# Modulation on four column groups of TensorE, its gate part beside the last tokens, norms one group ahead

## The chip, the cores and the metric

The kernel runs on one core of one Trainium2 chip. The core has five engines with their own instruction streams: TensorE (PE in the profile; its weight loads are listed apart as PEld), VectorE (DVE), ScalarE (ACT), GpSimd (POOL) and SyncE (SP). In this kernel SP issues all the transfers between the chip's memory and the core's SBUF. The metric is the time of one execution on the device, in microseconds; a time is the median of several executions. Each engine works through its stream in order, and an instruction that waits holds up all that stand behind it on its engine.

## What is computed

One layer of a streaming encoder, for 2048 prompt tokens and 8 sample streams of 16 tokens with a cache of 512 each, all of width 1024. Cut to what the change touches:

```python
def adaln_modulate(x, c, norm_g, w_ada, b_ada):
    mod = c @ w_ada + b_ada
    shift, scale, gate = jnp.split(mod, 3, axis=-1)
    h = rms_norm(x, norm_g) * (1.0 + scale[:, None, :]) + shift[:, None, :]
    return h, gate[:, None, :]

h, gate = adaln_modulate(xp, c_prompt, norm_g[l], w_ada[l], b_ada[l])
qa, ka, va, za, qb, kb, vb, zb, ga, gb = project_inputs(h, w_in[l], pos_p)
...
xp = xp + gate * merge_branches(oa, ob, za, zb, ga, gb, ...)
```

Here `c` has 9 rows (one for the prompt, eight for the sample streams), and `w_ada` is 1024 by 3072. Shift and scale (the first 2048 columns) are needed before any token can be projected. The gate (the last 1024) is used only where the output is made, at the end of the layer. Between the two stand the projections, differential attention and stick-breaking attention, and the merge.

## The kernel before

The program has an opening, a long loop and an output stage. The loop runs over 8 units (a unit is one head of differential attention, or two of stick-breaking attention) and over 17 tiles of 128 tokens, of which tile 16 is the sample tokens. For each step it projects one tile with the unit's weights and scores an earlier one. The projection's matmuls form one long list, `line`; `take(target, need)` cuts off the next pieces of it, and `interleave` merges several lists of pieces by their costs.

What is written in the program is a priority, not yet the order that runs. A planner at build time (`schedule_with_timeline_sim=True`) puts each engine's instructions in order by this priority and by when it expects them to be ready, and hands out the buffers of a pool as they come free. So the trace shows some work well ahead of its place in the program: the weights of unit 1 (`wst`, line 298) are requested at 32.83 us, while the opening runs until 160 us.

The opening (lines 875 to 1076) makes the modulated tokens in five groups: `GROUPS` 0 to 3 of 512 prompt tokens, and group 4 of the 128 sample tokens.

- Lines 903 to 910: the 9 rows of `c` are turned by TensorE so that their 1024 features lie on the partitions, and copied to `cT`, 8 blocks of 128 by 9. `bgT` has the biases and norm weights, turned in the same way.
- `modulation(n, p)`, lines 912 to 923: makes 512 columns of `c @ w_ada`. The weights come in two loads of 1 MB into `wide` buffers. There are 6 of those (`WIDE_BUFS`), and they hold the tokens, too: two tiles of 128 tokens to a buffer. Per half, 8 matmuls with `cT[:, k, :]` as the stationary operand add up into 9 rows of an accumulator bank. VectorE copies the 9 rows out, and four small transposes put them back with features on the partitions, into the bank `p`.
- Lines 925 to 936: `modulation` for n = 0 to 2, then loads and scales of unit 0's weights, then n = 3, then the loads of the tokens of groups 4 and 0 (`load_x`, line 893).
- Lines 938 to 994: factors of the attention and, from the modulation's first four blocks, the table `ab` of factors and offsets (lines 972 to 974), and a common scale `sh` (line 991) from their sizes.
- `normed(g)`, lines 996 to 1007: loads the group's tokens, ACT squares and adds up each tile (`sum_squares`, line 251), VectorE takes the root (`rsqrt`, lines 227 to 244: three rounds of four small steps), and GpSimd multiplies each tile by it in place (line 1007).
- `modulated(g)`, lines 1009 to 1041: eight pieces, one for each block of 128 features. TensorE transposes up to four tiles (line 1022), ACT (line 1028) and VectorE (line 1029) apply `ab` into a high part and a full one, and GpSimd or VectorE takes the difference for the low part (line 1037). With the last piece the group is stored to `hT_d` (line 1039); the copy in SBUF, `hp`, serves the first projections (`at_hand`).
- `gates()`, lines 1043 to 1066: `modulation` for n = 4 and 5 and then the gate's rows, turned back and stored to `gate_d` (line 1057). The output stage reads them from there (line 1214).
- Lines 1068 to 1076 set the order: norms of groups 4 and 0, group 4, then group 0 with `gates()` beside it, then the norm of group 1, and for groups 1 to 3 each group beside projections of unit 0 (up to tile positions `P0_AT`), and after it the norm of the next.

After the opening its pool is closed, and the loop's score buffers take over its memory.

Of the kernel before, what the change touches and what calls it, by code (L numbers as in the profile page):

```python
# [16 lines left out]
F32 = mybir.dt.float32  # L17
# [29 lines left out]
P0_AT = 2.0, 4.0, 6.0  # L47
# [45 lines left out]
def interleave(*streams):  # L93

    order = []
    for i, pieces in enumerate(streams):
        lo, hi = 0.0, 1.0
        if isinstance(pieces, tuple):  # L100
            pieces, lo, hi = pieces
        total = sum(cost for cost, _ in pieces) or 1.0
        done = 0.0
        for j, (cost, fn) in enumerate(pieces):
            order.append((lo + (hi - lo) * (done + cost / 2) / total, i, j, fn))
            done += cost
    for _, _, _, fn in sorted(order, key=lambda e: e[:3]):
        fn()
# [3 lines left out]
def layer_kernel(ctx: ExitStack, tc: tile.TileContext, a: dict):  # L112
    nc = tc.nc
    V, S, G, T = nc.vector, nc.scalar, nc.gpsimd, nc.tensor
# [112 lines left out]
    def rsqrt(sums, n, width, pool, name):  # L227

        m, tag = (4, "rs") if n <= 4 else (n, f"rs{n}")
        kw = {} if n <= 4 else dict(bufs=1)  # L230
        q = tiny.tile([P, m], F32, tag=tag + "_q", name="rs_q", **kw)[:, 0:n]
        V.tensor_scalar(out=q, in0=sums, scalar1=1.0 / width, scalar2=EPS, op0=ALU.mult, op1=ALU.add)
        i = tiny.tile([P, m], I32, tag=tag + "_i", name="rs_i", **kw)[:, 0:n]
        V.tensor_scalar(out=i, in0=q.bitcast(I32), scalar1=1, scalar2=None, op0=ALU.logical_shift_right)
        y = pool.tile([P, m], I32, tag=name, name=name)[:, 0:n]
        V.tensor_scalar(out=y, in0=i, scalar1=-1.0, scalar2=1597463007.0, op0=ALU.mult, op1=ALU.add)
        y = y.bitcast(F32)
        t = tiny.tile([P, m], F32, tag=tag + "_t", name="rs_t", **kw)[:, 0:n]
        for _ in range(3):
            V.tensor_tensor(out=t, in0=y, in1=y, op=ALU.mult)  # L240
            V.tensor_tensor(out=t, in0=t, in1=q, op=ALU.mult)  # L241
            V.tensor_scalar(out=t, in0=t, scalar1=-0.5, scalar2=1.5, op0=ALU.mult, op1=ALU.add)
# [612 lines left out]
    def position(x):  # L855

        m = min(int(x), len(steps) - 1)
        return starts[m] + (starts[m + 1] - starts[m]) * (x - m)

    def take(target, need):  # L860

        i = at[0]
        out = []
        while i < len(line) and (i < target or any(m <= need for m, _ in line[i : i + 14])):
            out.append((1.0, line[i][1]))
            i += 1
        at[0] = i
        return out
# [5 lines left out]
    ab = con.tile([P, 2, KT, 9], F32, name="ab")  # L874
    with tc.tile_pool(name="p0", bufs=1) as p0:
# [27 lines left out]
        pt = bank("t")  # L903
        for k in range(KT):
            T.transpose(pt[:, k * 16 : k * 16 + 9], cs[0:9, k * P : (k + 1) * P], ident[0:9, 0:9])
        T.transpose(pt[:, 128:160], bg, ident[0:32, 0:32])
        cT = p0.tile([P, KT, 9], F32, name="cT")
        V.tensor_copy(out=cT, in_=pt[:, 0 : KT * 16].rearrange("p (k r) -> p k r", r=16)[:, :, 0:9])
        bgT = p0.tile([P, 32], F32, name="bgT")
        V.tensor_copy(out=bgT, in_=pt[:, 128:160])  # L910

        def modulation(n, p):

            pw = bank("mm")
            for i in range(2):
                wa = wide_tile()
                load(out=wa, in_=w_ada[:, :, n * 512 + i * 256 : n * 512 + (i + 1) * 256])
                for k in range(KT):
                    T.matmul(pw[0:9, i * 256 : (i + 1) * 256], cT[:, k, :], wa[:, k, :], start=(k == 0), stop=(k == KT - 1))
            ms = p0.tile([P, 512], F32, tag="tmp", name="tmp", bufs=2)  # L920
            V.tensor_copy(out=ms[0:9, :], in_=pw[0:9, :])
            for j in range(4):
                T.transpose(p[:, j * 16 : j * 16 + 9], ms[0:9, j * P : (j + 1) * P], ident[0:9, 0:9])

        pm = bank("o")
        xs = {}
        for n in range(3):
            modulation(n, pm[:, n * 64 : (n + 1) * 64])
# [3 lines left out]
        modulation(3, pm[:, 192:256])  # L932
        for fn in early[4:] + late0:
            fn()
        xs[4] = load_x(16, 1)
# [28 lines left out]
        pmv = pm[:, 0:256].rearrange("p (j r) -> p j r", r=16)  # L964
# [7 lines left out]
        V.tensor_tensor(out=ab[:, 0, :, :], in0=pmv[:, 8:16, 0:9], in1=wide(b1), op=ALU.add)  # L972
        V.tensor_tensor(out=ab[:, 0, :, :], in0=ab[:, 0, :, :], in1=wide(bgT[:, 24:32]), op=ALU.mult)
        V.tensor_tensor(out=ab[:, 1, :, :], in0=pmv[:, 0:8, 0:9], in1=wide(bgT[:, 0:8]), op=ALU.add)

        mcol = p0.tile([P, 2], F32, name="mcol")
        V.tensor_reduce(out=mcol[:, 0:1], in_=ab[:, 0, :, :].rearrange("p k r -> p (k r)"), axis=AX.X, op=ALU.max,
# [16 lines left out]
                        scalar1=sh[:, 0:1], scalar2=None, op0=ALU.mult)  # L994

        def normed(g):

            t0, w = GROUPS[g]
            nt = w // P
            ss = p0.tile([P, 4], F32, tag="ss", name="ss", bufs=2)  # L1000
            if g not in xs:
                xs[g] = load_x(t0 // P, nt)
            for i, x in enumerate(xs[g]):
                sum_squares(x, D, ss[:, i : i + 1])
            rstd = rsqrt(ss[:, 0:nt], nt, D, p0, "rstd")
            for i, x in enumerate(xs[g]):
                G.tensor_scalar(out=x, in0=x, scalar1=rstd[:, i : i + 1], scalar2=0.0, op0=ALU.mult, op1=ALU.add)

        def modulated(g):

# [31 lines left out]

        def gates():

            box = {}

            def last():
                gateT = p0.tile([P, KT, 9], F32, name="gateT")
                V.tensor_tensor(out=gateT, in0=box["p"][:, 0:128].rearrange("p (j r) -> p j r", r=16)[:, :, 0:9],
                                in1=wide(bgT[:, 16:24]), op=ALU.add)  # L1050
# [6 lines left out]
                load(out=gate_d, in_=gr[0:9, 0:D])  # L1057

            def piece(n):
                if n == 4:  # L1060
                    box["p"] = bank("t")
                modulation(n, box["p"][:, (n - 4) * 64 : (n - 3) * 64])
                if n == 5:
                    last()

            return [(1.0, lambda n=n: piece(n)) for n in (4, 5)]

        normed(4)
        normed(0)
        interleave(modulated(4))  # L1070
        interleave(modulated(0), gates())
        normed(1)
        for g in range(1, 4):
            interleave(modulated(g), take(position(P0_AT[g - 1]), -1))
            if g < 3:
                normed(g + 1)


    at_hand.clear()
# [260 lines left out]
```

## Time and profile before

| | |
|---|---|
| time, median of 3 runs | 2507.16 us (2504.18 to 2513.22) |
| the profiled execution | 2508.37 us |
| its span, first to last instruction | 2506.5 us |
| TensorE busy | 2195.5 us, 88% of the span |
| VectorE busy | 1793.3 us, 72% |
| ACT busy | 1602.7 us, 64% |
| GpSimd busy | 827.6 us, 33% |
| DMA engines' share, queue 1 | 76.6% |
| mean granted clock of TensorE | 0.940 |

A share of busy time is an average over the stages of the run, and a busy TensorE is not TensorE at its peak, as its matmuls are pipelined. A row of a view by line gives the line, engine and operation, what is written and read, shapes and count; behind the first bar stand the busy time and the mean length of one (ns), behind the second the idle time before and what ended it. A row of a view in order of time begins with the start and the length in us, and its bracket gives the idle time before it and what ended that. A row of a view by windows gives a stretch, its length, each engine's busy time with its instructions, the granted clock, the DMA share and GB/s.

### The profile page before, as it was taken

Reading aid. Unit: us, or ns where it says so; the run is one execution under the profiler, and the core shown is the slowest. Engines: PE = TensorE matmul, PEld = TensorE weight load, DVE = VectorE, ACT = ScalarE, POOL = GpSimd, SP = SyncE. Lnnn points to the kernel's source line nnn. Section 1 sums busy time; section 2 is a strip of 40 time slices with the busy share of each in tenths; the row PEclk is TensorE's granted clock in tenths of the full one; section 3 lists DMA queues with packets and bytes.
Section 4 is the critical chain, followed back from the end, with each engine's and each line's share of the span. In section 5 each row is a group of like instructions: output and inputs, shape, how many; then the busy total and the mean of one; then the engine's idle time right before and its main releaser. Section 6 shows DMA issues by size and latency. Waiting matters only on the chain. (4 is left out here: it accounts for less than half of the span.)

```text
span 2506.5 us, 45283 instructions
## 1 busy us (share of the span) xinstructions
PE 2195.5 (88%) x16366; PEld 1275.3 (51%) x16366; DVE 1793.3 (72%) x3762; ACT 1602.7 (64%) x3200; POOL 827.6 (33%) x671
## 2 busy tenths in 40 slices
PE   7859898899999988889989888999975788889997
PEld 3435555455655555556655555555543344444443
DVE  3577846877676678757577876656787888888765
ACT  2558757787767688657678876656775545445542
POOL 1543113354211244311034442102344454544422
PEclk8979999999999999999999999999985799899999
DMA  9578878998787899767679976656678989888531
GB/s 287 183 221 206 211 175 200 196 220 191 180 193 185 198 222 212 172 152 183 157 192 194 219 190 177 160 132 142 153 168 206 257 224 242 242 212 229 167 111 51
DMA packets 890994, 477.07 MB, mean 190 GB/s; under 512 B 540074, under 2 KB 842330, under 8 KB 890256
## 3 DMA queue, kind: packets, MB, share of 16 engines
q1 hardware_dynamic: 890768, 474.17, 76.6%
q8 instruction: 128, 2.10, 0.4%
q14 instruction: 98, 0.80, 0.1%
HBM read 272.94 MB, written 73.44 MB: 138 GB/s over the span
## 5 line engine op out<-in xcount | busy, mean ns | idle before, releaser
L409 PE MATMUL ps_mm<-wpair,hg 128*128 128x512 f16 x3120 | 789.7, 388 | 58.1 <-DMA hg<-hT_d 54.4
L594 POOL TENSOR_TENSOR sc_p<-sc_p,sc_n 128x127 f32<-128x127 f32 (+7 forms) x192 | 314.0, 1639 | 807.3 <-DVE sc_n L588 796.0
L409 PEld LDWEIGHTS <-hg 128*128 128x128 f16 x3120 | 281.9, 100 | 328.9 <-DMA hg<-hT_d 62.5
L476 PE MATMUL ps_t<-gw,hg 128*128 128x256 f16 (+1 forms) x2856 | 397.6, 293 | 2.3 <-DVE qst L504 2.3
L476 PEld LDWEIGHTS <-hg 128*128 128x128 f16 x2856 | 280.4, 100 | 96.0 <-DVE qst L504 2.6
L588 DVE TENSOR_TENSOR_SCAN sc_n<-ps_s,sc_n,zero_t 128x512 f32<-128x512 f32 x192 | 245.6, 1279 | 63.4 <-ACT ps_s L121 58.2
L611 PE MATMUL ps_s<-k,qst 128*128 128x512 f16 (+3 forms) x640 | 226.5, 355 | 53.3 <-DVE sc_n L588 41.2
L545 DVE TENSOR_TENSOR sc_n<-sc_p,sc_n 128x128 f16<-128x128 f32 (+7 forms) x192 | 229.7, 1201 | 39.2 <-ACT sc_n L544 38.8
L121 ACT ACTIVATE sc_p<-ps_s,usc 128x512 f32<-128x512 f32 (+3 forms) x320 | 205.0, 641 | 47.1 <-PE ps_s L612 25.6
L612 PE MATMUL ps_s<-k,qst 128*128 128x512 f16 (+3 forms) x640 | 226.3, 356 | 0.0
L1227 PE MATMUL ps_mm<-wb,uT 128*128 128x512 f16 x816 | 206.8, 407 | 20.5 <-DVE o L1125 12.5
L121 ACT ACTIVATE ps_s<-ps_s,usc 128x512 f32<-128x512 f32 (+3 forms) x328 | 199.9, 610 | 0.0
L1266 PE MATMUL ps_o<-wo,yT 128*128 128x512 f16 x816 | 193.0, 390 | 6.9 <-ACT wo L269 2.4
L663 PE MATMUL ps_o<-v,wt 128*128 128x128 f16 x1088 | 156.5, 226 | 39.8 <-DMA wt<-sc_n 39.7
L544 ACT CAST sc_n<-sc_p 128x128 f16<-128x128 f32 (+7 forms) x192 | 154.8, 813 | 49.5 <-POOL sc_p L594 48.7
L442 POOL TENSOR_TENSOR rot<-pr,rope 128x256 f32<-128x256 f32 x68 | 59.8, 879 | 351.8 <-ACT pr L423 293.7
L251 ACT ACTIVATE junk<-wst 128x1024 f16<-128x1024 f32 x124 | 131.6, 1062 | 47.2 <-DMA wst<-in_w_in_dram 17.4
L663 PEld LDWEIGHTS <-wt 128*128 128x128 f16 x1088 | 104.0, 102 | 90.3 <-DMA wt<-sc_n 49.7
L1227 PEld LDWEIGHTS <-uT 128*128 128x128 f16 x816 | 82.7, 104 | 125.3 <-issue 50.8
L530 DVE TENSOR_SCALAR_CACHE_REDUCE sc_n<-ps_s,usc 128x512 f32<-128x512 f32 (+3 forms) x160 | 106.6, 666 | 55.2 <-PE ps_s L615 34.2
L664 PE MATMUL ps_o<-v,wt 128*128 128x64 f16 x1088 | 145.2, 198 | 0.0
L530 DVE TENSOR_SCALAR_CACHE_REDUCE sc_p<-ps_s,usc 128x512 f32<-128x512 f32 (+3 forms) x160 | 106.5, 666 | 52.6 <-PE ps_s L612 41.7
(295 smaller groups left out, 4372.9 us busy)
## 6 DMA issues: line engine op xcount, KB each, us to landing
hg<-hT_d SPq DMA_DIRECT2D x130, 512.0 KB, 4.5
wst<-in_w_in_dram SPq DMA_DIRECT2D x112, 256.0 KB, 3.8
g<-g_d SPq DMA_DIRECT2D x34, 512.0 KB, 5.8
wst<-in_w_in_dram SPq DMA_DIRECT2D x32, 512.0 KB, 4.8
out_dram<-pr SPq DMA_DIRECT2D x204, 64.0 KB, 2.3
g_d<-gt SPq DMA_DIRECT2D x102, 128.0 KB, 3.1
wide<-in_w_ada_dram SPq DMA_DIRECT2D x12, 1024.0 KB, 10.3
z_d<-pr SPq DMA_DIRECT2D x136, 64.0 KB, 1.8
```

Of the source, the lines that this page charges most:

```text
L121: i = S.activation(**kw)
L409: T.matmul(box["p"], box["h"][:, hi, k, :], U["w"][k][:, wi, :], start=(n == 0), stop=(n == 3 * KT - 1))
L476: T.matmul(box["g"][:, 0:gw], box["h"][:, hi, k, :], U["wg"][k // per][:, k % per, wi, :], start=(j == 0), stop=(j == 3 * KT - 1))
L530: V.tensor_scalar(out=dst[:, lo : lo + n], in0=p[:, 0:n], scalar1=sc_pos, scalar2=None, op0=ALU.mult, op1=ALU.max, accum_out=job["mx"][:, ...
L545: V.tensor_tensor(out=lo, in0=src, in1=hi, op=ALU.subtract)
L588: V.tensor_tensor_scan(out=dst[:, lo : lo + n][:, ::-1], data0=src[:, 0:n][:, ::-1], data1=zero_t[:, 0:1].to_broadcast([P, n]), initial=fi ...
L594: G.tensor_tensor(out=p[:, 0:m], in0=p[:, 0:m], in1=n[:, 1 : m + 1], op=ALU.mult)
L611: T.matmul(p[:, 0:n], qst[:, c, :], kk[:, c, 0:n], start=True, stop=False)
L612: T.matmul(p[:, 0:n], qst[:, 2 + c, :], kk[:, c, 0:n], start=False, stop=not diag)
L663: T.matmul(po[:, c * P : (c + 1) * P], wt[:, wj, :], vt[:, c, :, :], start=first, stop=False)
L1227: T.matmul(pb, st["u"][:, ui * 8 + br * 4 + k, :], wb[:, br, wi, k, c], start=(n == 0), stop=(n == 11))
L1266: T.matmul(po, st["y"][:, yi * 8 + k, :], wo[:, wi, k, c], start=(n == 0), stop=(n == 3 * KT - 1))
```

## The change

- `cT` gets 32 columns in each block instead of 9, the others zero (a memory set ahead of the copy).
- `modulation(n)` spreads the 8 matmuls of a half over four groups of 32 columns of TensorE: block k goes to group k % 4, so two matmuls add up in each group, and the bank holds four partial sums below one another. VectorE copies all 128 rows; four full transposes follow, into a bank of their own; and a VectorE reduction adds the four partial sums into the new tile `mod`, from which `ab` and the gate are then read. The bank `pm` that held the blocks is gone.
- `gates()` goes from beside group 0 to beside group 3.
- `normed(g)` returns pieces (a square for each tile, with the root after the last, then a multiplication for each tile) instead of issuing them. They are interleaved with the group ahead: group 1's norm with the pieces of group 0, and so on. `gates()` takes that place beside group 3.

```diff
-        cT = p0.tile([P, KT, 9], F32, name="cT")
-        V.tensor_copy(out=cT, in_=pt[:, 0 : KT * 16].rearrange("p (k r) -> p k r", r=16)[:, :, 0:9])
+        cT = p0.tile([P, KT, 32], F32, name="cT")
+        V.memset(cT, 0.0)
+        V.tensor_copy(out=cT[:, :, 0:9], in_=pt[:, 0 : KT * 16].rearrange("p (k r) -> p k r", r=16)[:, :, 0:9])
...
+        mod = p0.tile([P, 24, 9], F32, name="mod")
+
-        def modulation(n, p):
+        def modulation(n):
...
-                    T.matmul(pw[0:9, i * 256 : (i + 1) * 256], cT[:, k, :], wa[:, k, :], start=(k == 0), stop=(k == KT - 1))
+                    T.matmul(pw[k % 4 * 32 : k % 4 * 32 + 32, i * 256 : (i + 1) * 256], cT[:, k, :], wa[:, k, :], start=(k < 4), stop=(k >= 4))
             ms = p0.tile([P, 512], F32, tag="tmp", name="tmp", bufs=2)
-            V.tensor_copy(out=ms[0:9, :], in_=pw[0:9, :])
+            V.tensor_copy(out=ms, in_=pw)
+            pt = bank("s")
             for j in range(4):
-                T.transpose(p[:, j * 16 : j * 16 + 9], ms[0:9, j * P : (j + 1) * P], ident[0:9, 0:9])
-
-        pm = bank("o")
+                T.transpose(pt[:, j * P : (j + 1) * P], ms[:, j * P : (j + 1) * P], ident)
+            V.tensor_reduce(out=mod[:, 4 * n : 4 * n + 4, :], in_=pt.rearrange("p (j g r) -> p j r g", g=4, r=32)[:, :, 0:9, :],
+                            axis=AX.X, op=ALU.add)
...
-            for i, x in enumerate(xs[g]):
-                sum_squares(x, D, ss[:, i : i + 1])
-            rstd = rsqrt(ss[:, 0:nt], nt, D, p0, "rstd")
-            for i, x in enumerate(xs[g]):
-                G.tensor_scalar(out=x, in0=x, scalar1=rstd[:, i : i + 1], scalar2=0.0, op0=ALU.mult, op1=ALU.add)
+            return [(0.5, lambda i=i: square(i)) for i in range(nt)] + [(1.0, lambda i=i: scale(i)) for i in range(nt)]
...
-        normed(4)
-        normed(0)
+        interleave(normed(4))
+        interleave(normed(0))
         interleave(modulated(4))
-        interleave(modulated(0), gates())
-        normed(1)
+        interleave(modulated(0), normed(1))
         for g in range(1, 4):
-            interleave(modulated(g), take(position(P0_AT[g - 1]), -1))
-            if g < 3:
-                normed(g + 1)
+            beside = normed(g + 1) if g < 3 else gates()
+            interleave(modulated(g), beside, take(position(P0_AT[g - 1]), -1))
```

In the new `normed`, `square(i)` and `scale(i)` hold the same instructions as the two loops did, with the root behind the last square. In `gates()`, `box["p"]` and its reading are replaced by `mod[:, 16:24, :]`.

More of the change, by code (lines that the diff above doesn't have):

```diff
@@ L931, in layer_kernel @@
             fn()
-        modulation(3, pm[:, 192:256])
+        modulation(3)
         for fn in early[4:] + late0:
@@ L963, in layer_kernel @@
         V.tensor_scalar(out=g8, in0=g8, scalar1=1.0 - LAM_INIT, scalar2=None, op0=ALU.mult)
-        pmv = pm[:, 0:256].rearrange("p (j r) -> p j r", r=16)
         b1 = p0.tile([P, 8], F32, name="b1")
@@ L970, in wide @@
             return x.unsqueeze(2).to_broadcast([P, KT, 9])
-        V.tensor_tensor(out=ab[:, 0, :, :], in0=pmv[:, 8:16, 0:9], in1=wide(b1), op=ALU.add)
+        V.tensor_tensor(out=ab[:, 0, :, :], in0=mod[:, 8:16, :], in1=wide(b1), op=ALU.add)
         V.tensor_tensor(out=ab[:, 0, :, :], in0=ab[:, 0, :, :], in1=wide(bgT[:, 24:32]), op=ALU.mult)
-        V.tensor_tensor(out=ab[:, 1, :, :], in0=pmv[:, 0:8, 0:9], in1=wide(bgT[:, 0:8]), op=ALU.add)
+        V.tensor_tensor(out=ab[:, 1, :, :], in0=mod[:, 0:8, :], in1=wide(bgT[:, 0:8]), op=ALU.add)
         mcol = p0.tile([P, 2], F32, name="mcol")
@@ L999, in normed, with square, scale @@
             nt = w // P
-            ss = p0.tile([P, 4], F32, tag="ss", name="ss", bufs=2)
+            box = {}
+            def square(i):
+                if i == 0:
+                    box["ss"] = p0.tile([P, 4], F32, tag="ss", name="ss", bufs=2)
+                sum_squares(xs[g][i], D, box["ss"][:, i : i + 1])
+                if i == nt - 1:
+                    box["r"] = rsqrt(box["ss"][:, 0:nt], nt, D, p0, "rstd")
+            def scale(i):
+                x = xs[g][i]
+                G.tensor_scalar(out=x, in0=x, scalar1=box["r"][:, i : i + 1], scalar2=0.0, op0=ALU.mult, op1=ALU.add)
             if g not in xs:
                 xs[g] = load_x(t0 // P, nt)
-            for i, x in enumerate(xs[g]):
-                sum_squares(x, D, ss[:, i : i + 1])
-            rstd = rsqrt(ss[:, 0:nt], nt, D, p0, "rstd")
-            for i, x in enumerate(xs[g]):
-                G.tensor_scalar(out=x, in0=x, scalar1=rstd[:, i : i + 1], scalar2=0.0, op0=ALU.mult, op1=ALU.add)
+            return [(0.5, lambda i=i: square(i)) for i in range(nt)] + [(1.0, lambda i=i: scale(i)) for i in range(nt)]
         def modulated(g):
@@ L1043, in gates @@
         def gates():
-            box = {}
             def last():
                 gateT = p0.tile([P, KT, 9], F32, name="gateT")
-                V.tensor_tensor(out=gateT, in0=box["p"][:, 0:128].rearrange("p (j r) -> p j r", r=16)[:, :, 0:9],
+                V.tensor_tensor(out=gateT, in0=mod[:, 16:24, :],
                                 in1=wide(bgT[:, 16:24]), op=ALU.add)
@@ L1059, in piece @@
             def piece(n):
-                if n == 4:
-                    box["p"] = bank("t")
-                modulation(n, box["p"][:, (n - 4) * 64 : (n - 3) * 64])
+                modulation(n)
                 if n == 5:
```

2 lines of the change are left out of this document (1 added, 1 removed).

## The prediction

> **What bounds the kernel now.** I read the span and the engine totals first, then the whole run in windows of 100 us, and then the opening stretch in finer windows, in order of time and by line.
>
> ```profile
> span 2506.5 us, 45283 instructions
> PE 2195.5 (88%) x16366; PEld 1275.3 (51%) x16366; DVE 1793.3 (72%) x3762; ACT 1602.7 (64%) x3200; POOL 827.6 (33%) x671
> ```
>
> ```profile
> 0.00:100.00 100.00, 78.74 (x361) 35.27 (x362) 38.81 (x140) 32.49 (x63) 23.76 (x34) 0.92 0.76 244
> 100.00:200.00 100.00, 71.00 (x405) 40.42 (x404) 68.34 (x173) 63.64 (x141) 51.84 (x54) 0.82 0.68 212
> ...
> 700.00:800.00 100.00, 92.20 (x756) 60.32 (x754) 62.78 (x154) 69.35 (x153) 9.05 (x12) 1.00 0.80 192
> ```
>
> The columns are stretch, length, then busy time of PE, PEld, DVE, ACT and POOL, the granted clock, the DMA share and GB/s. From 200 us on the run is close to TensorE's own pace (92.20 of 100 in the last row). The first 160 us are not: TensorE is busy there, but with the modulation, and then everything waits in turn. All that the change touches lies in that opening. What it saves there moves the rest of the run forward, so I ask how much earlier the opening ends.
>
> The opening has three parts. In the first the modulation's weights arrive and are multiplied.
>
> ```profile
> 8.99 14.30 PE L919 MATMUL ps_mm<-wide,cT 128*9 128x256 f32 x56 [3.04 <-DMA wide<-in_w_ada_dram]
> ...
> 31.69 0.38 SPq L917 DMA_DIRECT2D wide<-in_w_ada_dram  x1
> 32.46 0.33 SPq L404 DMA_DIRECT2D rope<-in_shapes_dram  x1
> 32.83 5.70 SPq L298 DMA_DIRECT2D wst<-in_w_in_dram  x4
> 38.63 1.03 SPq L917 DMA_DIRECT2D wide<-in_w_ada_dram  x1
> ...
> 39.69 5.68 PE L919 MATMUL ps_mm<-wide,cT 128*9 128x256 f32 x16 [0.92 <-DMA wide<-in_w_ada_dram]
> 46.37 3.62 PE L919 MATMUL ps_mm<-wide,cT 128*9 128x256 f32 x16 [1.00 <-DMA wide<-in_w_ada_dram]
> 50.03 0.68 DVE L921 COPY tmp<-ps_mm 9x512 f32<-9x512 f32 x1 [0.24 <-PE ps_mm L919]
> ```
>
> Everything that follows needs the fourth block of products, which ends at 46.37 + 3.62 = 49.99 us. It started late because its second half was issued on SP's queue at 38.63 us, behind four loads of unit 1's weights. So a load, not TensorE, is last here. In the second part (56 to 108 us) TensorE is full and VectorE is not; in the third it is the other way round.
>
> ```profile
> 50.00:160.00 110.00, 80.62 (x416) 43.88 (x416) 72.67 (x191) 61.28 (x120) 63.83 (x67) 0.84 0.61 209
> 120.00:160.00 40.00, 19.53 (x105) 13.34 (x105) 34.78 (x61) 24.00 (x44) 28.56 (x29) 0.70 0.61 198
> ...
> 56.00:96.00 40.00, 39.59 (x193) 18.25 (x194) 17.59 (x52) 13.90 (x29) 16.23 (x19) 0.94 0.47 163
> ```
>
> ```profile
> L409 PE MATMUL ps_mm<-wpair,hp 128*128 128x512 f16 x107 | 25.6, 396 | 3.2 <-DVE v L274 3.2
> L919 PE MATMUL ps_mm<-wide,cT 128*9 128x256 f32 x64 | 17.2, 420 | 0.0
> ```
>
> The second fence is 56 to 108 us by line: 17.2 us of it is the gate part of the modulation, standing on TensorE in front of the transposes of tokens 0 to 511. The other delay of that part is on SP:
>
> ```profile
> 86.60 1.33 SPq L900 DMA_DIRECT2D wide<-in_x_prompt_dram  x3
> ...
> 107.98 0.28 PE L1022 MATMUL ps_s<-ident,wide 128*128 128x128 f32 x1
> ...
> 160.19 0.34 SPq L1039 DMA_DIRECT2D hT_d<-hp  x1
> ```
>
> The tokens of group 1 are not even requested before 86.60 us, since the gate's four weight blocks hold the `wide` buffers, and the first transpose of that group comes at 107.98 us. The opening ends at 160.19 us, when the last group's result is sent off.
>
> **The change, part by part.** *Products on four column groups.* There are 192 records of L919, two for each of 96 products. The nearest row for column groups is L735, whose 32 products run on four groups of 32 columns; a product of the same length on the full width is L409.
>
> ```profile
> 1984.47 1.91 PE L735 MATMUL ps_s<-dks,qpad 128*32 128x512 f16 x32
> ...
> 77.34 4.49 PE L409 MATMUL ps_mm<-wpair,hp 128*128 128x512 f16 x20
> ```
>
> That is 1.91/32 = 0.060 us each against 4.49/20 = 0.224, a ratio of 0.27. These are f16 and L919 is f32, so the bounds are 0.27 and 1; I take 0.27, because the form of the operands (32 columns, four groups in turn) is the same. The last half block then takes 3.62 x 0.27 = 1.0 us: 2.6 us earlier. Added per block are four full transposes instead of four small ones, and a reduction on VectorE:
>
> ```profile
> 113.63 0.60 PE L1022 MATMUL ps_s<-ident,wide 128*128 128x128 f32 x4
> 50.76 0.41 PE L923 MATMUL ps_o<-ident,tmp 9*128 9x9 f32 x4 [0.77 <-DVE rs_t L242]
> 51.83 0.23 DVE L977 TENSOR_REDUCE mcol<-ab 128x1 f32<-128x72 f32 x1
> ```
>
> The transposes cost 0.2 us more. The reduction reads 144 numbers from the accumulator, twice those of L977: 0.3 us, within 0.2 and 0.5. The copy of 128 rows costs what that of 9 rows does, as its 512 columns set it. The memory set of `cT` is done while the first weights travel (the products start only at 8.99 us). Net for this part: 2.6 - 0.5 = **2.1 us** earlier. The lower bound is a loss of 0.5 (no overlap of the groups). The upper bound is 12: with loads that never pause, 8.4 MB of weights for four blocks and 2.1 MB of unit 0's weights take 30 us from 6 us on at this rate, so the block could end at 38.
>
> ```profile
> 10.00:12.00 2.00, 2.00 (x7) 0.64 (x5) 0.00 (x0) 0.00 (x0) 0.00 (x0) 1.00 1.10 349
> ```
>
> I keep 2.1, since the pause comes from the order on SP, and that order is not touched.
>
> *Gate part moved to the last group.* It takes 64 records with their 17.2 us, two copies, and four 1 MB loads out of 43 to 76 us; SP then passes directly from group 0's tokens to group 1's, so the buffers hold tokens some 40 us sooner. What limits groups 0 to 3 after that is VectorE's and GpSimd's work. VectorE has 72.67 us of it between 50 and 160; where it ran densest, from 120 to 160, it was busy 34.78 of 40, or 87%. At that density the work takes 72.67/0.87 = 83.5 us. GpSimd's 63.83 at its own density there (28.56 of 40, 71%) takes 89. I take the middle, 87, against 110: **23 us** gained. TensorE needs 80.62 - 17.16 x 0.73 = 68 us in those 87, which fits (the row below is L919 alone, TensorE and its weight loads).
>
> ```profile
> 50.00:160.00 110.00, 17.16 (x64) 5.72 (x64) 0.84 0.61 209
> ```
>
> Bounds: 27 by VectorE alone, and 6 if every group takes as long as those from 108 to 160 did (52 us for three; at that pace the four groups and the sample tokens, counted as half a group, need 78, and the 25.6 us of projections that were done before 108 come on top: 104).
>
> *The gate's tail.* From the copy of the last products to the gate's store on SP, before took 9.3 us; on the way lie eight transposes and two copies, and after it the queue is free for the first loads of the attention.
>
> ```profile
> 79.98 0.68 DVE L921 COPY tmp<-ps_mm 9x512 f32<-9x512 f32 x1
> ...
> 89.25 0.30 SPq L1057 DMA_DIRECT2D gate_d<-wide  x1
> ```
>
> At the end of the opening this lies between wholly beside group 3 (0) and wholly behind it (9.3). I take **3 us** lost, a third, since TensorE was busy only 9.56 of the 18 us of group 3 but VectorE 14.31.
>
> ```profile
> 142.00:160.00 18.00, 9.56 (x49) 7.56 (x48) 14.31 (x26) 7.76 (x12) 12.70 (x12) 0.59 0.61 209
> ```
>
> *Roots and divisions one group ahead.* Here I give nothing. The order that is run already takes them ahead: the roots of group 3 stand at 122 to 140 us, amid the pieces of groups 1 and 2. Costed at 0, with bounds of 0 and a loss of 7 (below).
>
> ```profile
> 48.00:62.00 14.00, 4.09 (x24) 0.76 0.96 327
> 96.00:111.00 15.00, 6.11 (x24) 0.89 1.00 388
> 122.00:141.00 19.00, 6.20 (x12) 0.78 0.62 194
> ```
>
> These are the root's inner steps alone (tile `rs_t`, VectorE's busy time): 0.17 us a step where GpSimd is quiet, 0.52 beside its subtractions.
>
> The Trainium skill ("TensorE: Matmul & The Clock Gate", Part 1, the section on oscillation) says that short bursts between waits for loads run at half clock. This trace agrees where the fourth block starts after a pause: 5.68 us for 16 records against 3.62. By that rule the last half block is 1.5 instead of 1.0 us, and the sum is half a microsecond later.
>
> Sum: 2.1 + 23 - 3 = 22 us. The profiled execution took 2508.4 us (its span is 2506.5, with 1.9 around it), 1.2 above the median of 2507.2. **Forecast: 2508.4 - 22 = 2486 us.**
>
> **Rivals.** *Loads move up too* (0.13). If the freed buffers and the shorter products let the planner place the second half of block four ahead of unit 1's weights, the first part gains 12 instead of 2.1: 2476 us. For it speaks that the DMA engines were nearly idle for some 5 us just then, against it that the four loads in front need neither.
>
> ```profile
> 32.00:34.00 2.00, 0.81 (x4) 0.18 (x2) 0.26 (x1) 1.20 (x3) 0.00 (x0) 1.00 0.15 38
> ```
>
>
> *Roots get slower* (0.10). When all of groups 1 to 3 have their roots beside GpSimd's subtractions, two more chains of 12 steps cost 0.52 instead of 0.25: 6.3 us of VectorE, 7 at its density: 2493. The last row above speaks for it, that the planner did so already against it. The Trainium skill ("SBUF — State Buffer", Who interferes with whom) has a reason: a VectorE operation with two SBUF inputs and a GpSimd one that reads SBUF block each other for a whole instruction. The 0.52 agrees.
>
> *The groups do not overlap in f32* (0.12). Then 17.2 us of gate products stand at group 3, where TensorE has 18 - 9.56 = 8.4 us free: 8.8 behind it, with half of the tail (4.7) and the 0.5 of above. 23 - 14 = 9 gained: 2499.
>
> *The gain is given back later* (0.11). After 160 us TensorE, VectorE and ACT are at 124.78, 107.31 and 107.24 of 140.
>
> ```profile
> 160.00:300.00 140.00, 124.78 (x842) 68.51 (x843) 107.31 (x314) 107.24 (x246) 31.92 (x36) 0.94 0.80 214
> ...
> L409 PE MATMUL ps_mm<-wpair,hp 128*128 128x512 f16 x38 | 9.5, 380 | 3.0 <-POOL hp L1037 2.9
> ```
>
> If the 35.1 us of projections (L409, 25.6 before 108 us and 9.5 from there to 160) no longer fit beside the groups and half fall behind, 18 of 22 are lost: 2504.
>
> *Slower: TensorE waits in its order for the gate's loads* (0.12). Their four buffers come free only as groups 1 and 2 are transposed. A load into these buffers took up to 12.3 us to land in this stage (shortest, median, longest):
>
> ```profile
> DMA to landing us min/median/max: 5.2/7.8/12.3
> ```
>
> If each of the two gate pieces is planned before its load is in, the transposes of group 3 wait behind it twice, 24.6 us, and the tail of 9.3 follows whole: 23 + 2 - 34 = 9 lost, 2517 us. It decides from the point where the loads are issued less than a landing ahead of the products. For it: the products take the place of work that waited for nothing. Against: DMA has room from 110 us on.
>
> **How the numbers follow.** The forecast has 0.42 (its own range 2478 to 2494). Faster by over 0.3%, which is 7.5 us and about what a measurement here can tell from no change: the forecast, the first two rivals and a little under half of the third (0.05), 0.70. Within 0.3%: the fourth and as much of the third, 0.17. Slower: the last and what little of the third lies beyond, 0.13. The range 2469 to 2508 leaves out the slower case and the tail of the first rival.
>
> **What would show it.** Right: the end of L919's fourth block at 47 to 48 us, 16 of its records in about 1 us; requests for group 1's tokens before 60 us; VectorE busy 17.59 of 40 turned to over 30 of 40 in 56 to 96; the last hT_d store near 138 us; gate products beside group 3. Wrong: L919 at 0.21 us a record; TensorE idle on gate weights after 110 us; or a last store that is early while the end of the run is not.

## The result, and the profile after

| | before | after |
|---|---|---|
| median | 2506.03 us (17 runs, 2496.20 to 2513.22) | 2494.65 us (17 runs, 2488.39 to 2503.91) |
| ratio, 95% interval | | 0.9956 (0.9942 to 0.9970) |
| the profiled execution, its span | 2508.37 us, 2506.5 | 2503.67 us, 2501.9 |
| last store of the opening | 160.19 us | 138.57 us |

The change makes the kernel 11 us faster, 0.44%. The opening ends 21.6 us earlier, as forecast; half of that does not reach the end. The page of the changed kernel, span and busy times:

```profile
span 2501.9 us, 45310 instructions
PE 2162.8 (86%) x16366; PEld 1263.7 (51%) x16366; DVE 1807.2 (72%) x3769; ACT 1602.2 (64%) x3200; POOL 833.8 (33%) x671
```

TensorE has 33 us less to do (2195.5 before), and its share of the span falls from 88% to 86%: most of the work saved has turned into waiting. First the opening. SyncE's stream there, in order of time (start, length, what is issued):

```profile
25.83 0.58 SPq L922 DMA_DIRECT2D wide<-in_w_ada_dram  x1
...
29.85 0.38 SPq L922 DMA_DIRECT2D wide<-in_w_ada_dram  x1
...
39.52 6.56 SPq L900 DMA_DIRECT2D wide<-in_x_prompt_dram  x9
...
95.22 0.38 SPq L922 DMA_DIRECT2D wide<-in_w_ada_dram  x1
...
117.23 0.33 SPq L1053 DMA_DIRECT2D hT_d<-hp  x1
134.95 0.30 SPq L1069 DMA_DIRECT2D gate_d<-wide  x1
138.57 0.34 SPq L1053 DMA_DIRECT2D hT_d<-hp  x1
```

The last weights of block four are requested at 29.85 us, 8.8 earlier than before (38.63). Nine loads of tokens, all of groups 0 and 1 among them, are issued between 39.52 and 46.08 (group 1 before: 86.60). The gate's loads come at 95 us. The fourth of the five groups (group 2) is stored at 117.23, the last (group 3) at 138.57. TensorE's and VectorE's streams at the places that matter:

```profile
16.80 1.07 PE L924 MATMUL ps_mm<-wide,cT 128*32 128x256 f32 x16 [1.11 <-DMA wide<-in_w_ada_dram]
...
39.40 1.93 PE L924 MATMUL ps_mm<-wide,cT 128*32 128x256 f32 x16 [4.41 <-DMA wide<-in_w_ada_dram]
...
106.54 1.07 PE L924 MATMUL ps_mm<-wide,cT 128*32 128x256 f32 x16
...
121.33 1.07 PE L924 MATMUL ps_mm<-wide,cT 128*32 128x256 f32 x16
...
132.33 1.88 PE L1067 MATMUL ps_s<-ident,gateT 128*9 128x128 f32 x8
134.00 1.06 PE L1036 MATMUL ps_s<-ident,wide 128*128 128x128 f32 x4
```

```profile
41.40 0.69 DVE L926 COPY tmp<-ps_mm 128x512 f32<-128x512 f32 x1 [0.23 <-PE ps_mm L924]
...
127.41 0.68 DVE L926 COPY tmp<-ps_mm 128x512 f32<-128x512 f32 x1
...
135.91 0.81 DVE L1043 TENSOR_SCALAR tmp<-ps_s,ab 128x512 f32<-128x512 f32 x1 [0.98 <-ACT hp L1042]
```

Sixteen records take 1.07 us instead of 3.62. The block that sets the end of the first part is copied at 41.40 instead of 50.03. The gate's products have no wait ahead of them (no bracket). The last transposes of group 3 (134.00) stand behind the gate's own (132.33), so VectorE comes to group 3's last piece only at 135.91.

The same by windows (stretch, length, busy time of PE, PEld, DVE, ACT, POOL, clock, DMA share, GB/s):

```profile
38.00:42.00 4.00, 1.93 (x16) 0.59 (x16) 3.77 (x7) 0.00 (x0) 0.00 (x0) 0.50 1.13 319
...
56.00:96.00 40.00, 27.90 (x144) 14.62 (x144) 34.70 (x71) 30.29 (x56) 31.63 (x31) 0.96 0.55 189
```

Between 56 and 96 us VectorE is busy for 34.70 of 40 us (17.59 before), and TensorE for 27.90 (39.59 before). The middle of the opening has become VectorE's, as the prediction asked.

Then the loop, from the first to the 129th load of a head's tokens (`hg`, line 386), which is the same work in each kernel. Before, and after:

```profile
160.60:1798.50 1637.90, 1494.51 (x11422) 916.44 (x11421) 1151.22 (x2424) 1169.80 (x2474) 454.03 (x387) 0.97 0.79 186
```

```profile
139.00:1787.80 1648.80, 1495.52 (x11422) 916.03 (x11421) 1154.39 (x2426) 1168.38 (x2474) 454.96 (x387) 0.97 0.79 185
```

The same 11422 matmuls, the same busy time within 1 us, the same clock, and 10.9 us more. TensorE does not work longer: it waits 153.3 instead of 143.4 us. The loss is not at the seam with the opening. The lead over the kernel before is 22.6 us at load 32 (523 us) and nothing at load 48 (741 us), and then part of it comes back: 10.7 at load 128. The order in which the instructions stand on their engines differs from before between 200 and some 1000 us and in the output stage (from 1900 us on); from 1100 to 1800 us it is the same.

### The profile page after: what moved, and what is told of

Its sections match the earlier page's. It is cut to its first block, busy times and chain, and to the rows that moved or that the text cites. A ratio compares the mean times of both kernels' runs of the same rounds, so it can differ in the third digit from the quotient of the medians.

```text
span 2501.9 us, 45310 instructions
## 1 busy us (share of the span) xinstructions
PE 2162.8 (86%) x16366; PEld 1263.7 (51%) x16366; DVE 1807.2 (72%) x3769; ACT 1602.2 (64%) x3200; POOL 833.8 (33%) x671
## 4 chain that ended last, share of the span: by engine, by line
PE 40%; DMA 19%; DVE 16%; ACT 9%; issue 8%; POOL 4%; SPq 3%; DVEq 0%; POOLq 0%; ACTq 0%
PE ps_mm L409 16%; PE ps_t L476 9%; DMA hg<-hT_d 5%; DMA wt<-sc_n 4%; DMA wst<-in_w_in_dram 3%; DVE sc_n L588 3%; PE ps_s L611 2%; PE ps_mm L1235 2%; PE ps_s L612 2%; ACT junk L251 2%; ACT sc_p L121 2%; PE ps_o L1274 2%; DVE sc_n L545 1%; ACT ps_s L121 1%; DVE o L1127 1%
## 5 line engine op out<-in xcount | busy, mean ns | idle before, releaser
L611 PE MATMUL ps_s<-k,qst 128*128 128x512 f16 (+3 forms) x640 | 228.1, 358 | 52.4 <-DVE sc_n L588 41.3
L1235 PE MATMUL ps_mm<-wb,uT 128*128 128x512 f16 x816 | 200.0, 398 | 21.4 <-DVE o L1133 13.0
L663 PE MATMUL ps_o<-v,wt 128*128 128x128 f16 x1088 | 162.3, 228 | 42.4 <-DMA wt<-sc_n 42.4
L664 PE MATMUL ps_o<-v,wt 128*128 128x64 f16 x1088 | 150.6, 200 | 0.0
```

The lines of the kernel that those rows point to most:

```text
L611: T.matmul(p[:, 0:n], qst[:, c, :], kk[:, c, 0:n], start=True, stop=False)
L663: T.matmul(po[:, c * P : (c + 1) * P], wt[:, wj, :], vt[:, c, :, :], start=first, stop=False)
L1235: T.matmul(pb, st["u"][:, ui * 8 + br * 4 + k, :], wb[:, br, wi, k, c], start=(n == 0), stop=(n == 11))
```

## The experiments

What decides how long the loop is? The first eight runs went out under three theories. **A**: the planner's order of the loop is chance, and any small edit moves the time by 3 to 10 us. **B**: the loop can't start earlier, something else is late. **C**: the gate part at the end of the opening makes the planner reorder units 1 to 4, and this costs some 10 us.

**Null edits.** One memory set of 128 by 1 more, in both kernels.

```diff
     V.memset(zero_t, 0.0)
+    spare_t = con.tile([P, 1], F32, name="spare_t")
+    V.memset(spare_t, 0.0)
```

> The kernel before, with one more memory set of 128x1 on VectorE at the start (about 0.06 us of work) and nothing else. The opening should end at 160 us as before (within 3). Theory A (half of the 22 us that the change gained in the opening was given back because the planner puts the loop's instructions in another order, and that order is good or bad by accident): the order in the loop comes out different here too, and the time moves by 3 to 10 us to one side or the other. Theory B (the loop itself cannot start earlier, whatever its order): no change, within 2 us of before.

> The changed kernel with the same additional memory set of about 0.06 us. The opening should end at 139 us (within 3). Theory A: the time lies 3 to 10 us away from the changed kernel's 2494.7, to one side or the other (2485 to 2505), with another order in the loop. Theory B: 2494.7 within 2 us.

Measured against the kernel before: 1.0004 (0.9991 to 1.0016) and 0.9975 (0.9960 to 0.9989). Each trace has its parent's order of instructions on every engine. A falls in this form: the order is not disturbed by a trifle. Two kernels of one order still differ: the second gains some 5 us less than the change with its 0.9956 (the intervals overlap; B allowed 2), and its opening ends 3 us later (141.53), so a single trace gives the end of an opening only to some 3 us.

**The gate part put elsewhere in the changed kernel.** Back beside group 0 (as before, with both other parts kept), beside group 2, beside group 1:

```diff
-        interleave(modulated(0), normed(1))
+        interleave(modulated(0), gates(), normed(1))
...
-            beside = normed(g + 1) if g < 3 else gates()
+            beside = normed(g + 1) if g < 3 else []
```

> The changed kernel, but the gate part stands beside group 0 again (products on column groups and norms ahead are kept). If holding the token buffers was the cost of the gate part's old place, the requests for group 1's tokens come after 60 us again and the opening ends at 148 to 156 us, time 2500 to 2505. If the cost was TensorE's 17 us alone, which column groups cut to under 5, the opening ends at 135 to 142 and the time is 2490 to 2498.

```diff
-            beside = normed(g + 1) if g < 3 else gates()
-            interleave(modulated(g), beside, take(position(P0_AT[g - 1]), -1))
+            beside = normed(g + 1) if g < 3 else []
+            interleave(modulated(g), beside, gates() if g == 2 else [], take(position(P0_AT[g - 1]), -1))
```

> The changed kernel with the gate part one group earlier, beside group 2 in place of group 3. In the changed kernel's trace group 3's last two pieces stand behind the gate's tail. If that tail is what holds the end of the opening, the opening ends at 128 to 133 us in place of 138.6; if the tail only filled time, at 137 to 140. The total: theory A gives 2480 to 2500 with no close tie to the opening's end; theory B gives 2494.7 within 2 us in both cases; a loop that starts with the opening's end and runs as in the changed kernel gives 2485 to 2488.

> The changed kernel with the gate part beside group 1. Its four buffers are then asked of groups 4 and 0. Theory C with the end of the opening as the cause: the gate's store leaves some 50 us before the loop, the loop's order is as before again and the opening's gain is passed on whole; opening's end 140 to 150, ratio 0.991 to 0.995. If it is any place but the old one that changes the loop's order: opening 140 to 150 and ratio 0.995 to 1.000.

The last has `g == 1` in that line. Measured: 0.9941 (0.9924 to 0.9958), 0.9993 (0.9978 to 1.0008) and 0.9971 (0.9957 to 0.9986). The first is the surprise: its opening gains only 12.9 us, 9 less than the change, and it is not slower than the change. Its loop takes 1636.9 us and its lead of 11 to 17 us stays to the end, so B falls. From 200 to 1800 us its instructions stand in the order of the kernel before, on every engine. For its opening neither forecast came true: it ends at 147.3 us, between the two windows, although group 1's tokens are requested at 42.5 already. With the gate part beside group 2 the opening (150.3) missed both of its windows, too. Beside group 1 it came as expected (145.3), with the ratio of the second case there, "any place but the old one".

**Each part alone, in the kernel before.** Column-group products; norms one group ahead (gate part beside group 0); gate part beside group 3. The diffs are those parts of the change; the last:

```diff
-        interleave(modulated(0), gates())
+        interleave(modulated(0))
...
-            interleave(modulated(g), take(position(P0_AT[g - 1]), -1))
+            interleave(modulated(g), gates() if g == 3 else [], take(position(P0_AT[g - 1]), -1))
```

> The products on column groups alone; the gate part stays beside group 0 and the norms are issued as before. With e3 (this and the norms ahead) the opening ended at 147.3 us, 12.9 before the kernel before. If the norms ahead bring nothing, since the planner takes them ahead anyhow, the opening ends at 146 to 149 here too, and the ratio is 0.993 to 0.996. If they brought half of it, 153 to 155 and 0.996 to 0.999. The loop's order from 200 to 1800 us: as before in both cases.

> The norms one group ahead alone; products and gate part as before. If the planner did it already: opening ends at 158 to 162, ratio 0.998 to 1.002. If it is half of e3's gain: 153 to 155, ratio 0.996 to 0.999.

> The gate part moved beside group 3 alone; its products on the full width, norms as before. The forecast's view (buffers and TensorE freed for groups 0 and 1): the opening ends at 140 to 152 us. Theory C (from e3 and e4: a gate part at the end of the opening makes the planner order units 1 to 4 of the loop in another way, which costs some 10 us there; at group 0 it leaves the loop as it was): the loop's order differs from before between 200 and 1000 us, and the loop's part of e7 is 5 to 15 us longer than before's, so that the ratio is 0.996 to 1.002. Against C: the loop's order is as before and the whole gain is passed on, ratio 0.991 to 0.996.

Measured: 0.9961 (0.9947 to 0.9975), 1.0034 (1.0022 to 1.0047), 0.9990 (0.9972 to 1.0009). Every one shortens the opening (the first head load comes 8.4, 6.5 and 10.0 us earlier), and yet the second is slower than before. The third came as C says (another order, a loop 5.5 us longer than before's 1637.9). The first missed what I expected of its order: it is not that of before, but a third one. The second has the opening of "half of the gain" (153.7), but a ratio above both of its windows. Its gate part is where it always was, and the order of its loop is the changed kernel's from 300 us on but for a few instructions, so C as it stood falls too: the order matters, but it is not the gate's place that makes it.

That left **D**: the order in the loop, fixed by where the planner stands at the end of the opening, sets the loop's length, whatever the opening gained. Its rival **E**: a loop that starts earlier gives time back in any order. Both are told apart by the changed kernel with its short opening and another order, and moving the gate's pieces within group 3 does that.

```diff
-            beside = normed(g + 1) if g < 3 else gates()
+            beside = normed(g + 1) if g < 3 else (gates(), 0.2, 1.0)
```

> The changed kernel with one number more: the gate part's two pieces are spread over the last 0.2 to 1.0 of group 3's work instead of 0 to 1. The instructions of GpSimd and VectorE in the loop then stand in the kernel before's order, to the last one in the stretch of units 1 to 5, as they did with the gate part back beside group 0. Theory D (the order of the engines' instructions in the loop, fixed by where the planner stands at the end of the opening, decides how long the loop is, and the chip then only follows it): opening ends 136 to 145, first to last head-group load 1635 to 1642 us as in the kernel before (1637.9) and with the gate part back (1636.9), end 2486 to 2498, ratio 0.990 to 0.9945. Theory E (a loop that starts some 20 us earlier gives 10 us back whatever its order, for instance because its loads collide with the opening's last stores): loop 1647 to 1651 us as in the changed kernel (1648.8), ratio 0.995 to 0.998.

The other two have `0, 0.5` and `0.3, 0.9` there.

> The changed kernel with the gate part's two pieces in the first half of group 3's work (0 to 0.5) instead of the whole of it, so that the gate's copies, sum and store come ahead of group 3's last pieces. Order in the loop: that of the changed kernel on GpSimd to the last instruction, on VectorE for about 94 of 100. If the gate's tail holds up the opening's last store, this store comes at 126 to 136 instead of 138.6 to 141.5; if the tail only changes places with the last pieces, it stays at 138 to 142. Theory D: loop 1645 to 1652 us all the same, so ratio 0.993 to 0.9975. Theory E: the earlier the opening ends, the more is given back: loop 1650 to 1660 us, ratio 0.9955 to 1.000.

> The changed kernel with the gate part's two pieces between 0.3 and 0.9 of group 3's work. In units 1 to 5 GpSimd's instructions then stand in the order of the kernel with the column-group products alone, to the last one, VectorE's for 99 of 100: a third order, whose loop took 1638.3 us. Theory D: the short opening of the changed kernel (last store 137 to 146) and that loop (1634 to 1642 us) together, so ratio 0.987 to 0.9935. Theory E (a short opening is paid back in any order but one that happened to be good in the run with the spread gate part): loop 1643 to 1651 us, ratio 0.9945 to 0.999.

The fourth run is the change without the norms ahead:

```diff
-        interleave(modulated(0), normed(1))
+        interleave(modulated(0))
+        normed(1)
         for g in range(1, 4):
-            beside = normed(g + 1) if g < 3 else gates()
-            interleave(modulated(g), beside, take(position(P0_AT[g - 1]), -1))
+            interleave(modulated(g), gates() if g == 3 else [], take(position(P0_AT[g - 1]), -1))
+            if g < 3:
+                normed(g + 1)
```

> Column-group products and the gate part beside group 3, the norms where the kernel before has them. Its order in the loop is that of the changed kernel on GpSimd to the last instruction in units 1 to 5, but it has none of the norms ahead. Opening by the parts measured alone (8.4 and 10.0 less than 160.2): last store at 141 to 150. Theory D: loop 1646 to 1652 us, ratio 0.996 to 1.001. Theory E, or a theory by which the norms ahead are what the loop pays for: loop 1636 to 1642 us, ratio 0.990 to 0.9945.

The spread gate part gives **0.9890** (0.9868 to 0.9911), 2475.23 us: the best version of all, from one pair of numbers. Its opening is the changed kernel's, its loop's order the one of before, and its loop:

```profile
138.80:1769.80 1631.00, 1492.85 (x11422) 916.48 (x11421) 1149.63 (x2426) 1170.34 (x2474) 455.22 (x387) 0.97 0.79 187
```

1631.0 us and 0.9890 lie a little below D's 1635 to 1642 us and 0.990 to 0.9945, and far from E's 1647 to 1651 and 0.995 to 0.998. The gate early gives 0.9979 (0.9963 to 0.9994): its loop (1646.0) is as D says, but its ratio lies just above D's 0.9975, and its opening ends not earlier, but 3.1 us later (141.7). It decides nothing on the gate's tail: the gate's store came only 1.1 us earlier than in the change (133.83), and 3 us is what two kernels of one order differ by here. The third order gives 0.9942 (0.9922 to 0.9963): a loop of 1640.2 us as D says, and a ratio just above D's 0.9935, with an opening that ends 5 us later than the change's.

The change without the norms ahead gives 0.9965 (0.9943 to 0.9988), with a loop of 1644.3 us, 1.7 short of D's window, and an opening that ends at 139.7, earlier than I expected. It could not do what it was made for: its five instruction streams are the changed kernel's, one by one. So it is a second sample of the changed kernel (the null edit is a third: 0.9956, 0.9965 and 0.9975), and it shows something else: with the gate part beside group 3, the edit "norms one group ahead" changes no instruction at all.

All runs together. The second column is how much earlier than before the first head load comes (traces). The third is the change of the time by the ratio, in us of the runs of before on the same chip. The fourth, their difference, is what the rest of the run lost (plus) or won. The last is the stretch from head load 32 to 48.

| kernel | opening | time | rest | loads 32 to 48 |
|---|---|---|---|---|
| *loop in the order of before* | | | | |
| before | 0 | 0 | 0 | 195.1 |
| before, null edit | -2.1 | +1.0 | +3.1 | 197.2 |
| gate back | -12.9 | -14.8 | -1.9 | 195.1 |
| gate spread 0.2 to 1 | -21.8 | -27.6 | -5.8 | 194.5 |
| *a third order* | | | | |
| column groups alone | -8.4 | -9.8 | -1.4 | 208.4 |
| gate 0.3 to 0.9 | -16.7 | -14.5 | +2.2 | 208.1 |
| gate beside group 2 | -9.8 | -1.8 | +8.0 | 206.3 |
| *the order of after* | | | | |
| after | -21.6 | -11.0 | +10.6 | 218.0 |
| after, null edit | -18.7 | -6.3 | +12.4 | 220.9 |
| after without norms ahead | -20.5 | -8.8 | +11.7 | 219.1 |
| gate 0 to 0.5 | -18.5 | -5.3 | +13.2 | 219.4 |
| norms ahead alone | -6.5 | +8.5 | +15.0 | 220.9 |
| *other orders* | | | | |
| gate late alone | -10.0 | -2.5 | +7.5 | 208.8 |
| gate beside group 1 | -14.9 | -7.3 | +7.6 | 212.7 |

The stretch's rows, one trace each: before, gate spread, column groups alone, gate 0.3 to 0.9, after, and norms ahead alone.

```profile
545.90:741.00 195.10, 181.73 (x1472) 116.55 (x1471) 135.32 (x337) 143.44 (x314) 56.90 (x54) 1.00 0.82 188
```

```profile
521.40:715.90 194.50, 181.37 (x1471) 116.61 (x1470) 134.80 (x336) 143.36 (x314) 56.95 (x54) 1.00 0.81 189
```

```profile
533.50:741.90 208.40, 185.30 (x1469) 117.50 (x1468) 141.38 (x341) 143.21 (x316) 55.99 (x55) 0.98 0.78 181
```

```profile
523.30:731.40 208.10, 185.70 (x1459) 117.46 (x1456) 141.51 (x341) 143.06 (x315) 55.82 (x54) 0.97 0.77 181
```

```profile
523.20:741.20 218.00, 194.57 (x1526) 122.11 (x1525) 149.16 (x361) 151.65 (x335) 55.53 (x54) 0.98 0.78 186
```

```profile
541.40:762.30 220.90, 196.46 (x1528) 123.35 (x1525) 149.59 (x361) 152.21 (x335) 54.58 (x54) 0.97 0.77 183
```

The reader is to compare the first two and the last two: kernels of one order agree in length, in the count of matmuls and in every engine's busy time, though their stretches begin up to 25 us apart, and kernels of two orders do not. The order of after does 54 matmuls more between the same two loads (1526 against 1472, some 13 us, which the two next stretches regain: 207.4 against 212.0 and 207.8 against 217.1) and waits 10 us longer (218.00 - 194.57 = 23.4 against 13.4). The wait that grew there is named by the view of waits of TensorE (total, times, longest), for the same stretch before and after:

```profile
PE ps_mm L409 <- DMA hg<-hT_d: 3.8, 3, 2.1
```

```profile
PE ps_mm L409 <- DMA hg<-hT_d: 14.2, 10, 2.7
```

In this stretch TensorE waits for the tokens of the head 10.4 us longer. This is not yet the cost of the order, for over the whole loop that wait is the same, before and after:

```profile
PE ps_mm L409 <- DMA hg<-hT_d: 54.4, 29, 5.7
...
PE ps_t L489 <- ACT gt L479: 5.0, 5, 1.9
```

```profile
PE ps_mm L409 <- DMA hg<-hT_d: 54.8, 35, 5.6
...
PE ps_t L489 <- ACT gt L479: 9.5, 8, 2.0
```

The 10 us that TensorE waits longer in the loop as a whole are spread over smaller waits: 4.5 for ACT's `gt`, 3.6 for VectorE's `sc_n` (26.3 against 22.7) and the rest in pieces of some 2 us that grow or shrink. So the stretch shows what the order does there; which wait makes the loop longer in the end is not shown.

E falls: the shortest opening of all goes with the shortest rest. D holds for the difference that the question was about: the rest goes from -6 to +3 us in the order of before and from +11 to +15 in the order of after, and the third order lies between, at -1 to +8. Within one order up to 9 us remain that D does not explain. Two pairs show this best, as from about 150 us to the end their instructions stand in the same order on every engine: gate back and gate spread (-1.9 and -5.8), gate beside group 2 and gate 0.3 to 0.9 (+8.0 and +2.2). A ratio's interval is 3 to 6 us to either side, which covers most of that, and the traces differ in the output stage, too (710.4 us with the gate back, 703.6 with the gate spread, from load 128 to the end). The two with the larger rest ran on one chip, their partners on two others; whether the chip makes the difference is not shown.

## Why the prediction was right, and where it was not

The time lies in the range and the sign is right, but the change gives 11 us where the forecast said 22. The step that failed is one sentence: "What it saves there moves the rest of the run forward". In its place the runs showed that the opening also fixes the planner's order of the loop, and that this order costs 11 to 15 us, with the same work in it. The signal I had named for it came ("a last store that is early while the end of the run is not"). With the order of before, the same opening gives 27.6 us.

**The sum itself** was right by luck: 22 against 21.6 measured, as the errors of its terms nearly cancel: the first gain came out 6.5 us larger than taken, the second 2.3 smaller, and the loss 4.8 larger. The rows that this needs from the kernel before and from the one with the gate back are their stores of the fourth and the last group:

```profile
146.60 0.34 SPq L1039 DMA_DIRECT2D hT_d<-hp  x1
...
160.19 0.34 SPq L1039 DMA_DIRECT2D hT_d<-hp  x1
```

```profile
133.66 0.33 SPq L1053 DMA_DIRECT2D hT_d<-hp  x1
...
147.28 0.34 SPq L1053 DMA_DIRECT2D hT_d<-hp  x1
```

- *Products on column groups*: 2.1 in the text, 8.6 measured (copy of block four at 41.40 instead of 50.03). The ratio was right: 1.07/3.62 = 0.30, I took 0.27. Wrong was "the pause comes from the order on SP, and that order is not touched": SyncE requested block four's halves 5.9 and 8.8 us earlier. That is the rival *Loads move up too*; it came true for 8.6 of its 12, and the forecast of the opening was saved by the next two terms. The size is that of these two traces: this copy stands at 48.1 to 50.0 us in the four kernels with products on the full width, and at 41.3 to 44.1 in the ten with column groups.
- *Groups beside each other*: 23 in the text. From the copy to the fourth group's store it took 117.23 - 41.40 = 75.8 us against 146.60 - 50.03 = 96.6: 20.7 gained. VectorE was as dense as supposed (82.46 of 98 us from 41 to 139, 84%), but had 10 us more to do in it.
- *The gate's tail*: a loss of 3 in the text, 7.8 measured: the last group takes 138.57 - 117.23 = 21.3 us, against 13.6 before, and 13.6 with the gate part back beside group 0. This is close to the full 9.3, but that the tail is all of it is not shown: of the 6.9 us that VectorE has more to do in this last group (18.11 against 11.17), the gate's two copies of products, two sums, one addition and two copies of rows are 3.6, and with the gate part beside group 1, stored at 105.33, the last group took 20.1 us as well.
- *Norms one group ahead*: 0 in the text, and exactly 0 where the gate is late, as no instruction moves. With the gate beside group 0 the edit does move the opening, by 6.5 alone.

8.63 + 20.74 - 7.75 = 21.62.

**The Trainium skill's rule** on short bursts ("TensorE: Matmul & The Clock Gate", Part 1, oscillation) speaks for the better of the two prices of the last half block. I had 1.0 us by the row and 1.5 by the rule. It took 1.93, after a wait of 4.41 us and at a granted clock of 0.50 in 38 to 42 us; the same 16 records took 1.07 after a wait of 1.11.

**The rivals.** *The groups do not overlap in f32* is refuted by 1.07 us. *TensorE waits for the gate's loads* is refuted: the first is requested at 95.22, 11.3 us ahead of its products, and no record of the gate's products has a wait. *Roots get slower* came in small: VectorE's time in the root's inner steps was 16.4 us before (4.09 + 6.11 + 6.20) and is 18.59 now; of the two chains that I had feared, one stands in this row at the price of 0.5 us a step:

```profile
85.00:100.00 15.00, 6.01 (x12) 0.89 0.98 324
```

*The gain is given back later* had the nearest kind of outcome, and 2494.65 lies midway between its 2504 and the forecast's 2486, but not its mechanism: it wanted the projections of unit 0 to fall behind right after the opening, and the lead is still whole (22.6 us) at 523 us.

**The verdict on the wait at the end of the opening** shows a trap. The same wait of GpSimd stands in the traces after and with the gate spread as

```profile
136.80 1.15 POOL L1051 TENSOR_TENSOR hp<-tmp,hp 128x512 f16<-128x512 f32 x1 [5.94 <-DMA gate_d<-wide]
```

```profile
136.66 1.15 POOL L1051 TENSOR_TENSOR hp<-tmp,hp 128x512 f16<-128x512 f32 x1 [6.98 <-DVE tmp L1043]
```

The store of the gate (134.95) is only the event next to it; what was late was `tmp`, whose transposes stood behind the gate's at 134.00.

**What stays open.** Why a given opening leads the planner to one order or another: that was not tried, and the place of the gate's pieces does not follow a pattern that I can see (0 to 1 and 0 to 0.5 give the order of after on GpSimd, 0.2 to 1 that of before, 0.3 to 0.9 the third). Nor is it shown which instruction of the order, or which of the waits, makes the loop longer. The planner hands out the buffers together with the order, and no run here separates the two: what is called the order above is its whole plan.

## What to carry to other kernels

Where a planner orders the instructions, an edit of the opening can reorder units that come long after it; compare the order of the two traces behind the edit before any gain or loss is put down to the edit itself. When an opening gets shorter and the end does not, try neighbouring placements of the same pieces: here one of them, at no cost, more than doubled the gain. And a sum that comes out right proves none of its terms: check each against the trace.

## What I had not expected of the hardware

- Column groups of 32 pay off in f32 as they do in f16: 16 records of 256 columns in 1.07 us against 3.62 (0.30), while the row for f16 gave 0.27.
- After a wait of 4.41 us for a load, these 16 records took 1.93 us, 1.8 times as long, at a granted clock of 0.50.
